# Row softmax on one core: tiles of 15, 7 and 3 rows per partition in place of 16, 8 and 4

## The chip, the core and the metric

The kernel runs on one NeuronCore of a Trainium2 chip. Its engines have instruction streams of their own and meet only at semaphores: VectorE (DVE in the profile) reduces and multiplies, ScalarE (ACT) computes exponentials, SyncE (SP) only issues transfers here. Sixteen DMA engines move data between HBM and the on-chip memory SBUF, which has 128 partitions. Transfers issued by ACT go through one queue (q10 in the profile), those issued by SP through another (q1); both run on the same sixteen engines. The metric is the device time of one execution in microseconds (us).

## The reference

A softmax over the last axis, at temperature 2, of 16 x 1024 rows of 512 float32 numbers:

```python
temp = 2.0
x_scaled = x / temp
x_max = np.max(x_scaled, axis=-1, keepdims=True)
exp_x = np.exp(x_scaled - x_max)
return exp_x / np.sum(exp_x, axis=-1, keepdims=True)
```

The input has 33.55 MB and so has the output; each is moved once. A row has 2 KB.

## The kernel before

There are 16,384 rows, 128 for each partition. A *tile* is a run of rows in HBM: tile t with r rows per partition takes 128 x r consecutive rows, and partition p gets the r consecutive ones from p x r on (`dram`, L54 to L56). A tile is therefore one contiguous stretch of HBM, cut into 128 pieces of r x 2 KB, and these pieces start r x 2 KB apart: with r = 16, the pitch from one partition to the next is 32 KB; with 8, 16 KB; with 4, 8 KB.

`PLAN` (L10) lists eleven tiles as (rows, place). The place is an offset in `arena`, an SBUF buffer of 100 rows per partition (L36), in which everything is computed in place. The first eight tiles (4, 8, five of 16, 8) fill the 100 rows exactly. The last three (16, 8, 4) reuse the places of tiles 2, 1 and 0; `behind` (L63 to L68) lists for each of them which earlier tile holds its place.

The work runs as follows.

- ACT issues the loads of the first eight tiles at the start (L81), one after another, and then computes.
- A *chunk* is 4 rows of a tile (`CHUNK`, L15), 32 in all. For chunk k, DVE takes the negated maximum of each row (L99, one instruction per chunk, `do_max`), ACT computes exp(0.5 x - max) row by row and accumulates the row's sum (L84, four instructions), and DVE takes the reciprocals (L108) and multiplies each row by its own (L112, `do_mul`).
- DVE's order is max(k), then mul(k - 2), since `LAG` is 2 (L121 to L125). The max of a tile's chunks waits for that tile's load.
- SP stores tile t when its last chunk is multiplied (L130, L131). After store t it issues the loads of late tiles whose place was held by tile t - 2 or an earlier one; each first waits for the store of that earlier tile (L132 to L136). In this plan all three late loads are issued after store 4. At the end SP waits for all stores (L137, L138).

SP's queue is first in, first out: a late load stands behind the stores issued before it.

Of the kernel before, what the change touches and what calls it, by code (L numbers as in the profile page):

```python
# [1 line left out]

# [4 lines left out]

PLAN = [  # L10
    (4, 0), (8, 4), (16, 12), (16, 28), (16, 44), (16, 60), (16, 76),
    (8, 92), (16, 12), (8, 4), (4, 0),
]
ARENA = 100
CHUNK = 4  # L15
LAG = 2


@with_exitstack
def kernel(  # L20
    ctx: ExitStack,
    tc: tile.TileContext,
    x: bass.AP,
    out: bass.AP,
):
    nc = tc.nc
    fp32 = mybir.dt.float32

    xf = x.flatten_outer_dims()
    of = out.flatten_outer_dims()  # L30
    N, D = xf.shape
    P = nc.NUM_PARTITIONS
    n_rows = N // P
    assert sum(r for r, _ in PLAN) == n_rows

    arena = nc.alloc_sbuf_tensor("arena", (P, ARENA, D), fp32)  # L36
    negmax = nc.alloc_sbuf_tensor("negmax", (P, n_rows), fp32)
    sums = nc.alloc_sbuf_tensor("sums", (P, n_rows), fp32)
    recip = nc.alloc_sbuf_tensor("recip", (P, n_rows), fp32)


    tiles, base = [], 0
    for r, at in PLAN:
        tiles.append((base, r, at))
        base += r

    chunks = [
        (t, b + c, at + c)
        for t, (b, r, at) in enumerate(tiles)
        for c in range(0, r, CHUNK)  # L50
    ]
    last_chunk = {t: k for k, (t, _, _) in enumerate(chunks)}

    def dram(ap, t):  # L54
        b, r, _ = tiles[t]
        return ap[b * P : (b + r) * P].rearrange("(p r) d -> p r d", r=r)  # L56

    def sb(t):
        _, r, at = tiles[t]
        return arena[:, at : at + r, :]  # L60


    behind = {}  # L63
    for t, (_, r, at) in enumerate(tiles):
        for u in range(t):
            _, ru, au = tiles[u]
            if at < au + ru and au < at + r:
                behind.setdefault(t, []).append(u)  # L68

    with tc.tile_critical():  # L70
        ld = [tc.alloc_semaphore(f"ld{t}") for t in range(len(tiles))]
        st = [tc.alloc_semaphore(f"st{t}") for t in range(len(tiles))]
        s_max = tc.alloc_semaphore("s_max")
        s_exp = tc.alloc_semaphore("s_exp")
        s_rec = tc.alloc_semaphore("s_rec")
        s_mul = tc.alloc_semaphore("s_mul")


        for t in range(len(tiles)):
            if t not in behind:  # L80
                nc.scalar.dma_start(out=sb(t), in_=dram(xf, t)).then_inc(ld[t], 16)  # L81
        for k, (t, b, a) in enumerate(chunks):
            for r in range(CHUNK):
                ins = nc.scalar.activation(  # L84
                    out=arena[:, a + r],
                    in_=arena[:, a + r],
                    func=mybir.ActivationFunctionType.Exp,
                    bias=negmax[:, b + r : b + r + 1],
                    scale=0.5,
                    accum_out=sums[:, b + r : b + r + 1],  # L90
                )
                if r == 0:
                    ins._wait_ge(s_max, k + 1)
            ins.then_inc(s_exp, 1)


        def do_max(k):
            t, b, a = chunks[k]
            nc.vector.reduce_max(  # L99
                out=negmax[:, b : b + CHUNK],  # L100
                in_=arena[:, a : a + CHUNK],
                axis=mybir.AxisListType.X,
                negate=True,
            )._wait_ge(ld[t], 16).then_inc(s_max, 1)

        def do_mul(k):
            t, b, a = chunks[k]
            nc.vector.reciprocal(  # L108
                out=recip[:, b : b + CHUNK], in_=sums[:, b : b + CHUNK]
            )._wait_ge(s_exp, k + 1).then_inc(s_rec, 1)  # L110
            for r in range(CHUNK):
                ins = nc.vector.tensor_scalar_mul(  # L112
                    out=arena[:, a + r],
                    in0=arena[:, a + r],
                    scalar1=recip[:, b + r : b + r + 1],
                )
                if r == 0:
                    ins._wait_ge(s_rec, k + 1)
            ins.then_inc(s_mul, 1)

        for k in range(len(chunks) + LAG):  # L121
            if k < len(chunks):
                do_max(k)
            if k >= LAG:
                do_mul(k - LAG)  # L125


        late = sorted(behind)
        for t in range(len(tiles)):
            nc.sync.wait_ge(s_mul, last_chunk[t] + 1)  # L130
            nc.sync.dma_start(out=dram(of, t), in_=sb(t)).then_inc(st[t], 16)  # L131
            while late and max(behind[late[0]]) <= t - 2:  # L132
                u = late.pop(0)
                for v in behind[u]:
                    nc.sync.wait_ge(st[v], 16)
                nc.sync.dma_start(out=sb(u), in_=dram(xf, u)).then_inc(ld[u], 16)  # L136
        for t in range(len(tiles)):  # L137
            nc.sync.wait_ge(st[t], 16)  # L138


# [1 line left out]
_INS = ['x']  # L142
_OUTS = [((16, 1024, 512), 'float32')]


# [23 lines left out]
```

The softmax here doesn't subtract the row's maximum and nothing guards it: scores larger than these inputs give would overflow.

## Time and profile before

| What | Value |
|---|---|
| device time, median of 4 runs | 164.23 us (163.81 to 165.01) |
| the profiled execution's own time | 163.81 us |
| its span | 162.0 us |
| moved by DMA | 67.14 MB, mean 414 GB/s over the span |
| DMA issues | 8 loads from ACT, 3 loads and 11 stores from SP |
| DVE max of a chunk (L99) | 32 x 2280 ns, 72.9 us |
| DVE multiply of a row (L112) | 128 x 482 ns, 53.6 us |
| ACT exponential of a row (L84) | 128 x 710 ns, 90.8 us |
| DVE waits for loads | 15.1 us in 5 waits, the first of them 5.64 us at the start |
| SP waits for DVE before stores | 133.2 us in 11 waits |

The durations come from one profiled execution, whose span runs from its first to its last recorded instruction; about 1.8 us of the device time lie around it. The page gives each engine's busy time, a row of forty slices in which a digit is the busy share in tenths, and for each DMA queue the number of packets, the megabytes and the time that its packets took, as a share of the span of sixteen engines. Busy times of neighbouring instructions on one engine can overlap by some tens of ns, so a sum over means can be a little above the time that passes. Idle time of an engine that does not set the end costs nothing.

### The profile page before, as it was taken

To read this page: it belongs to the slowest core of one execution; us is meant where nothing else is said; L and a number is where in the kernel's file an instruction comes from. 1 tells how busy PE (TensorE), PEld (TensorE's weight loads), DVE (VectorE), ACT (ScalarE), POOL (GpSimd) and SP (SyncE) were. 2 spreads that over 40 slices of the span, in tenths; PEclk is the share of its full clock that TensorE was granted. 3 is DMA by queue.
4 is the path that set the end of the run, shared out by engine and by line. 5 is a ranking of instruction groups with operands and counts; after the bars stand their busy time and mean duration, and the time that the engine had idled before them with its cause. 6 is when DMAs were issued, how large, how long until landed. Compare 5 with 4: busy or idle time off the path is not lost.

```text
span 162.0 us, 528 instructions
## 1 busy us (share of the span) xinstructions
DVE 127.0 (78%) x192; ACT 95.0 (59%) x257; POOL 0.2 (0%) x4
## 2 busy tenths in 40 slices
DVE  0539199999999999999985999998999999930000
ACT  0368537777777777777771777776777777700000
POOL 0000000000000000000000000000000000000000
DMA  5999989999999999999999999999999999999993
GB/s 166 433 437 502 404 344 459 453 417 396 421 483 396 445 445 404 437 421 437 413 453 409 441 425 443 421 429 400 417 429 445 445 413 407 429 461 429 400 423 148
DMA packets 3172, 67.14 MB, mean 414 GB/s; under 512 B 352, under 2 KB 352, under 8 KB 352
## 3 DMA queue, kind: packets, MB, share of 16 engines
q1 hardware_dynamic: 2016, 40.90, 59.1%
q10 hardware_dynamic: 1152, 26.21, 38.4%
q14 instruction: 4, 0.03, 0.0%
HBM read 33.55 MB, written 33.55 MB: 414 GB/s over the span
## 4 chain that ended last, share of the span: by engine, by line
DVE 54%; DMA 33%; issue 1%; ACTq 1%; SPq 0%
DMA arena<-in_x_dram 33%; DVE negmax L99 29%; DVE arena L112 24%; DVE recip L108 1%; ACTq L81 1%; SPq L131 0%; ACTq L164 0%; SPq L70 0%
## 5 line engine op out<-in xcount | busy, mean ns | idle before, releaser
L84 ACT ACTIVATE arena<-arena,negmax 128x512 f32<-128x512 f32 x128 | 90.8, 710 | 40.7 <-DVE negmax L99 40.7
L99 DVE TENSOR_REDUCE negmax<-arena 128x4 f32<-128x2048 f32 x32 | 72.9, 2280 | 15.1 <-DMA arena<-in_x_dram 15.1
L112 DVE TENSOR_SCALAR arena<-arena,recip 128x512 f32<-128x512 f32 x128 | 53.6, 482 | 1.1
L84 ACT ACTIVATION_READ_ACCUMULATOR arena<-arena,negmax 128x1 f32 x128 | 23.9, 187 | 0.0
L108 DVE RECIPROCAL recip<-sums 128x4 f32<-128x4 f32 x32 | 5.4, 168 | 0.0
L84 ACT ACT_TABLE_LOAD x1 | 1.3, 1283 | 5.1 <-issue 5.1
L153 POOL MEMSET const-bfloat16-1.0<- 128x1 bf16 x1 | 0.1, 101 | 0.0
L153 POOL MEMSET const-uint8-127<- 128x1 uint8 x1 | 0.1, 101 | 0.0
L153 POOL MEMSET const-float32-0.0<- 128x1 f32 x1 | 0.1, 98 | 0.2 <-issue 0.2
L153 POOL MEMSET const-float32-1.0<- 128x1 f32 x1 | 0.1, 98 | 0.0
## 6 DMA issues: line engine op xcount, KB each, us to landing
out_dram<-arena SPq DMA_DIRECT2D x6, 4096.0 KB, 26.2
arena<-in_x_dram ACTq DMA_DIRECT2D x5, 4096.0 KB, 44.7
out_dram<-arena SPq DMA_DIRECT2D x3, 2048.0 KB, 20.1
arena<-in_x_dram ACTq DMA_DIRECT2D x2, 2048.0 KB, 53.3
arena<-in_x_dram SPq DMA_DIRECT2D x1, 4096.0 KB, 34.7
out_dram<-arena SPq DMA_DIRECT2D x2, 1024.0 KB, 17.4
arena<-in_x_dram SPq DMA_DIRECT2D x1, 2048.0 KB, 38.3
arena<-in_x_dram ACTq DMA_DIRECT2D x1, 1024.0 KB, 4.7
```

The lines of the kernel that those rows point to most:

```text
L81: nc.scalar.dma_start(out=sb(t), in_=dram(xf, t)).then_inc(ld[t], 16)
L84: ins = nc.scalar.activation(out=arena[:, a + r], in_=arena[:, a + r], func=mybir.ActivationFunctionType.Exp, bias=negmax[:, b + r : b + r ...
L99: nc.vector.reduce_max(out=negmax[:, b : b + CHUNK], in_=arena[:, a : a + CHUNK], axis=mybir.AxisListType.X, negate=True,)._wait_ge(ld[t], ...
L108: nc.vector.reciprocal(out=recip[:, b : b + CHUNK], in_=sums[:, b : b + CHUNK])._wait_ge(s_exp, k + 1).then_inc(s_rec, 1)
L112: ins = nc.vector.tensor_scalar_mul(out=arena[:, a + r], in0=arena[:, a + r], scalar1=recip[:, b + r : b + r + 1],)
L153: nc = _bacc.Bacc("TRN2", target_bir_lowering=False, num_devices=1)
```

## The change

The plan now gives each tile as a list of chunk sizes: tiles of 3, 7, six of 15, and at the end 15, 7, 3 and 3 rows. A tile of 15 has three chunks of 5 rows, one of 7 a chunk of 4 and one of 3, and one of 3 a single chunk. There are twelve tiles instead of eleven and 28 chunks instead of 32. The pitch from one partition to the next in HBM becomes 30, 14 or 6 KB. The first eight tiles again fill the 100 rows of `arena`. The late tiles are now four: tile 8 in the place of tile 2, tile 9 in that of 1, tile 10 in that of 0, and tile 11 (3 rows) in part of that of tile 3, so its load is issued after store 5. A chunk carries its own size, and the loops run over it.

```diff
 PLAN = [
-    (4, 0), (8, 4), (16, 12), (16, 28), (16, 44), (16, 60), (16, 76),
-    (8, 92), (16, 12), (8, 4), (4, 0),
+    ([3], 0), ([4, 3], 3), ([5] * 3, 10), ([5] * 3, 25), ([5] * 3, 40), ([5] * 3, 55),
+    ([5] * 3, 70), ([5] * 3, 85), ([5] * 3, 10), ([4, 3], 3), ([3], 0), ([3], 25),
 ]
 ARENA = 100
-CHUNK = 4
 LAG = 2
...
-    tiles, base = [], 0
-    for r, at in PLAN:
+    tiles, chunks, base = [], [], 0
+    for t, (cs, at) in enumerate(PLAN):
+        r = sum(cs)
         tiles.append((base, r, at))
+        o = 0
+        for c in cs:
+            chunks.append((t, base + o, c, at + o))
+            o += c
         base += r
-
-    chunks = [
-        (t, b + c, at + c)
-        for t, (b, r, at) in enumerate(tiles)
-        for c in range(0, r, CHUNK)
-    ]
-    last_chunk = {t: k for k, (t, _, _) in enumerate(chunks)}
+    last_chunk = {c[0]: k for k, c in enumerate(chunks)}
...
+    def do_max(k):
+        t, b, c, a = chunks[k]
+        nc.vector.reduce_max(
+            out=negmax[:, b : b + c],
+            in_=arena[:, a : a + c],
+            axis=mybir.AxisListType.X,
+            negate=True,
+        )._wait_ge(ld[t], 16).then_inc(s_max, 1)
...
-        for k, (t, b, a) in enumerate(chunks):
-            for r in range(CHUNK):
+        for k, (t, b, c, a) in enumerate(chunks):
+            for r in range(c):
```

`do_mul` changes in the same way: its reciprocal takes c numbers and its loop runs over c rows. The rest of the diff puts the loads of ACT into a function `issue_loads` and the rest into `compute_and_store`, which are called one after the other; the order of issue on each engine follows the same rules as before.

More of the change, by code (lines that the diff above doesn't have):

```diff
@@ L33 @@
     n_rows = N // P
-    assert sum(r for r, _ in PLAN) == n_rows
+    assert sum(sum(c) for c, _ in PLAN) == n_rows
     arena = nc.alloc_sbuf_tensor("arena", (P, ARENA, D), fp32)
@@ L68, with issue_loads, do_mul, compute_and_store @@
                 behind.setdefault(t, []).append(u)
[L70 to L79, printed above, removed]
+    ld = [tc.alloc_semaphore(f"ld{t}") for t in range(len(tiles))]
+    st = [tc.alloc_semaphore(f"st{t}") for t in range(len(tiles))]
+    s_max = tc.alloc_semaphore("s_max")
+    s_exp = tc.alloc_semaphore("s_exp")
+    s_rec = tc.alloc_semaphore("s_rec")
+    s_mul = tc.alloc_semaphore("s_mul")
+    def issue_loads(begin, end):
+        for t in range(begin, end):
             if t not in behind:
                 nc.scalar.dma_start(out=sb(t), in_=dram(xf, t)).then_inc(ld[t], 16)
-        for k, (t, b, a) in enumerate(chunks):
-            for r in range(CHUNK):
+    def do_max(k):
[6 more added lines that the diff above has]
+        )._wait_ge(ld[t], 16).then_inc(s_max, 1)
+    def do_mul(k):
+        t, b, c, a = chunks[k]
+        nc.vector.reciprocal(
+            out=recip[:, b : b + c], in_=sums[:, b : b + c]
+        )._wait_ge(s_exp, k + 1).then_inc(s_rec, 1)
+        for r in range(c):
+            ins = nc.vector.tensor_scalar_mul(
+                out=arena[:, a + r],
+                in0=arena[:, a + r],
+                scalar1=recip[:, b + r : b + r + 1],
+            )
+            if r == 0:
+                ins._wait_ge(s_rec, k + 1)
+        ins.then_inc(s_mul, 1)
+    def compute_and_store():
+        for k, (t, b, c, a) in enumerate(chunks):
+            for r in range(c):
                 ins = nc.scalar.activation(
@@ L94 @@
             ins.then_inc(s_exp, 1)
[L97 to L119, printed above, removed]
         for k in range(len(chunks) + LAG):
@@ L138 @@
             nc.sync.wait_ge(st[t], 16)
+    with tc.tile_critical():
+        issue_loads(0, len(tiles))
+        compute_and_store()
 _INS = ['x']
```

## The prediction

> **What bounds the kernel now.** I read the page first: the engines' busy times, the forty slices and the DMA queues.
>
> ```profile
> span 162.0 us, 528 instructions
> DVE 127.0 (78%) x192; ACT 95.0 (59%) x257; POOL 0.2 (0%) x4
> ...
> DMA  5999989999999999999999999999999999999993
> ...
> q1 hardware_dynamic: 2016, 40.90, 59.1%
> q10 hardware_dynamic: 1152, 26.21, 38.4%
> ```
>
> VectorE (DVE) is busy 78% of the span. The DMA row is full from the second slice to the last but one, and the two queues' packets took 59.1 + 38.4 = 97.5% of sixteen engines' span: 158.0 of 162.0 us. The other 4 us are the head (the first packet starts at 1.8 us) and the tail (the last byte lands at about 160.2). So DMA sets the end, although the chain of waits names DVE for 54%: a chain runs through whatever happened to be waited for, and DVE ends at 143.2, with 17 us of stores still queued.
>
> Next, the stretches of the trace: us, length, busy DVE, ACT and POOL with instructions, clock, share of DMA engines busy, GB/s.
>
> ```profile
> 2.00:16.00 14.00, 7.69 (x7) 7.33 (x18) 0.00 (x0) 1.00 1.00 417
> 24.00:157.00 133.00, 114.96 (x180) 83.84 (x230) 0.00 (x0) 1.00 1.00 428
> 145.00:157.00 12.00, 0.00 (x0) 0.00 (x0) 0.00 (x0) 1.00 0.97 418
> ```
>
> Loads alone (first row), the mixture (second) and stores alone (third) all run with the engines full at 417 to 428 GB/s. One row per partition (128 x 2 KB) read or written therefore costs 262,144 B / 428 GB/s = 0.6125 us, and 256 such rows cost 156.8.
>
> Then the records of single packets in the trace. A packet is one partition's contiguous run, 8, 16 or 32 KB: 22 transfers x 128 = 2816 of them, plus 22 x 16 semaphore writes of 9 ns. The most frequent duration of each size is also its minimum: 309, 611 and 1213 ns, which 2500 of the 2816 take. Doubling a packet adds 302 or 602, so a packet costs some 7 ns besides its bytes. The time above these minima, summed and divided by 16 engines, is the whole **excess** any better address pattern could win: 2.09 us. It splits into the first 4-row load (before the engines have settled) 0.51, the last 4-row load (114.6 to 119 us; mean 364 instead of 309) 0.44, 32 KB loads 0.80 (20 ns each), 32 KB stores 0.32 (6 ns each), rest 0.02.
>
> **The change, part by part.** My sum stands against the profiled execution, 163.81 (span 162.0 and 1.8 around it); the median of the four runs is 164.23, and I add the same difference to that.
>
> *The pitch.* Tiles remain one contiguous run of HBM; only where each partition's piece starts in it changes, 30 KB apart instead of 32. The engines' least packet times do not depend on the pitch before: 8, 16 and 32 KB pieces all move at 27 GB/s per engine. Between 8.5 and 13.5 us, loads at 32 KB pitch with nothing beside them, no packet is above its minimum; at the end of the kernel the same holds for stores. Bounds: a gain of at most 2.09 - 0.51 = 1.58 (the start-up share is not a matter of pitch), a loss not bounded by a row. I take 0 for the big tiles, the value of the undisturbed stretches. A rule is worth weighing here. The Trainium skill ("DMA: Bandwidth & Descriptors", section "Latency and other measured facts") has copies losing rate at large power-of-two row pitches: 207 GB/s per direction at 512 KiB against 214 in full. Read as "any power of two costs this", it would promise 3.3% of 157, 5.2 us. But it starts at sixteen times our pitch, and names contiguous tiles as an alternative cure, which this kernel has already; and our steady 428 GB/s, half in each direction, is its full rate. The row decides: 1.58 at most, not 5.2.
>
> *More, smaller transfers.* 12 tiles instead of 11 make 24 transfers instead of 22: per engine 16 more packets at 7 ns and 2 semaphore writes at 9 ns, 0.13 us. Here a rule speaks against the change: the same page ("Anatomy of one DMA") charges some 2.0 us fixed per transfer, which would be 4 us for two. The trace has transfers queued behind one another: from 1.8 to 160.2 us, engines are idle 158.4 - 157.8 = 0.6 us on average over all 22. The fixed part lies beside other transfers' packets while a queue is never empty; so 0.13, not 4.
>
> *The small loads.* Before has one 4-row load late in a full queue, with 0.44 us of excess; after has two of 3 rows (tiles 10 and 11). Nearest row: another 0.44; if it was chance, 0. I take half, 0.22.
>
> *Compute.* 32 chunks become 28. Four rows take DVE 2.19 + 0.12 + 1.68 = 3.99 us (max; reciprocal and gaps; four multiplies, in the chain of waits), five at most 5/4 of max and multiply: 2.74 + 0.12 + 2.09 = 4.95, so 0.99 per row instead of 1.00. ACT needs about 0.71 x 5 = 3.5 of these. All of that lies beside DMA: worth 0, provided a queue always holds something. That needs checking, because loads and stores move.
>
> *The supply of the queues.* ACT's queue still gets 100 rows at the start (3 + 7 + 6 x 15), so its issue is the same eight instructions. SP's order becomes stores 0 to 4, loads 8, 9, 10, store 5, load 11, stores 6 to 11; load 11 (new) waits for store 3, which was issued about 30 us before. In the FIFO of rows, and 1.8 us for the start: tile 2 lands after 25 rows and 3 of store 0, at 19.0 us (before: 20.5). Store 2 then goes out 23.4 us of DVE later, at 42.4; by then 66 rows have moved, 10 of them stores. From there stores share evenly with loads (0.816 rows per us each), so 85 loaded rows stand at 78 and 100 at 96.3. The same sum for before gives 86.4 for its tile 6, measured:
>
> ```profile
> 86.95 2.29 DVE L99 TENSOR_REDUCE negmax<-arena 128x4 f32<-128x2048 f32 x1 [2.55 <-DMA arena<-in_x_dram]
> ```
>
> DVE wants tile 6 at 76.9 and tile 7 at 93.2 (three chunks of 4.95 after tile 6): it waits some 1.5 and 3.6 us, against 2.55 and 0.58 before, the second wait now at tile 7 because that tile has 15 rows, not 8. Tile 8 is wanted at 111.6 and lands at 106. DVE ends at about 144 (before 143.2). What matters is whether store 8 is issued before store 7 has drained. Before:
>
> ```profile
> 135.60 0.33 SPq L131 DMA_DIRECT2D out_dram<-arena  x1
> ```
>
> and stores to tile 7 drain at 1.8 + 228 x 0.6125 = 141.4: cover of 5.8 us. After: issued at 134.7, needed at 141.6, cover 6.9. Store 6: issued 106.7, needed 123. So no queue runs dry, DVE's new wait costs nothing, and a last store of 3 rows instead of 4 drains under the same tail.
>
> **Sum.** 0 (pitch) + 0.13 + 0.22 + 0 (compute) = +0.35: 163.81 becomes 164.16 in a profiled run, and 164.23 becomes 164.58. I forecast **164.5**, no change that can be told: about 0.5% (0.8 us) is what a measurement of this kernel can tell from none, with four runs 1.2 us apart. Its own range is 163.5 to 165.2.
>
> **Rivals.**
> *A, the pitch does cost.* The 32 KB loads' excess and the 4-row loads' late excess are collisions in HBM, and 30 and 6 KB pitches spread them: 164.23 - 1.58 + 0.13 = 162.8. For it: the excess sits in loads, at certain times, many packets at once. Against: long stretches at the same pitch have none, and 1.58 is the ceiling.
> *B, slower: the new pitch collides more.* Place: the 112 packets of 30 KB per engine (14 transfers x 8). Before, sixteen engines step through pieces a power of two apart; that may be the good pattern. If every 30 KB packet, stores too, gets the 20 ns of the 32 KB loads, excess of large tiles is 2.24 instead of 1.12; with 0.13 and 0.44 that is +1.7: 165.9. It decides from 6 ns more per packet (0.82 - 0.13 = 0.69 us over 112). For it: 8 KB loads in a full queue took 18% more at the one place where they occur. Against: stores at 8, 16 and 32 KB all sit on the minimum.
> *C, a queue runs dry.* If tile 7 comes 7 us later than I have it, store 8 is late and each further us is a us of the end: 10 us later, 167.6.
> *D, it does not do what it says.* If 30 KB does not go as one packet but in pieces of 16, 8, 4 and 2, three more per packet at 7 ns are 112 x 3 x 7 ns = 2.35 us: 166.9. Nothing in this trace shows a size that is not a power of two, so it cannot be excluded.
>
> **How the numbers follow.** Forecast 0.48 (0.45 of it within 0.5%, 0.03 slower), A 0.20, B 0.22, C 0.05, D 0.05. Faster 0.20, same 0.45, slower 0.35. The range 162.6 to 166.3 takes in A's 162.8 and B's 165.9 with some room and leaves out the far side of B, most of C and D.
>
> **What would show it.** In the changed profile: the DMA row full but for its ends, and 24 x 144 = 3456 packets in the two queues (D: more). Packets of 30 KB with a most frequent time of 7 + 30/32 x 1206 = 1138 ns, 6 KB near 234, 14 KB near 535, and an excess near 2.3 us (A: under 1; B: over 3). The steady rate 426 to 429 GB/s. DVE's waits for loads at tiles 6 and 7 near 1.5 and 3.6 us. Store 8 issued near 135 and no slice below 9 at 141 (C). The forecast is wrong if the packets' minima move, or if the shares fall below 9 tenths anywhere between the ends.

## The result, and the profile after

| | median | runs |
|---|---|---|
| before | 164.43 us (163.54 to 167.99) | 55 |
| changed | 163.61 us (163.0 to 164.32) | 36 |

The ratio is 0.9955, 95% interval [0.9943, 0.9967]: faster by 0.45%, some 0.74 us. A later run of the same pair (e11) gives 0.9959 [0.9939, 0.9978]. The ratios leave out slow executions such as the one of 167.99. The effect is small but clear of the noise, and the forecast of no change, at 164.5, missed its direction.

The two profiled executions do not show it: the one of before took 163.81, below its median, the one of after 163.95, above its own. A difference of 0.45% has to be read from several profiles and from the intervals.

Page of the changed kernel: busy times, the DMA row of the forty slices and the DMA queues.

```profile
span 162.2 us, 523 instructions
DVE 126.2 (78%) x184; ACT 94.5 (58%) x257; POOL 0.2 (0%) x4
...
DMA  5999999999999999999999999989999999999992
...
q1 hardware_dynamic: 2304, 40.90, 58.8%
q10 hardware_dynamic: 1152, 26.21, 38.4%
q14 instruction: 3, 0.02, 0.0%
```

DMA is as full as before. The packets are 3456, so 30 KB go as one packet; in the packet records the most frequent times are 1138 ns for 30 KB, 535 for 14 and 234 for 6. The excess that was forecast near 2.3 us is 1.53. One more row differs: q14, instruction, has 3 packets here and 4 before.

Of the compute side, two lines of the timeline of VectorE in the changed kernel (start, duration, what, idle time before it and its cause), and SyncE's issue of store 8:

```profile
78.59 2.82 DVE L85 TENSOR_REDUCE negmax<-arena 128x5 f32<-128x2560 f32 x1 [1.75 <-DMA arena<-in_x_dram]
96.88 2.82 DVE L85 TENSOR_REDUCE negmax<-arena 128x5 f32<-128x2560 f32 x1 [3.41 <-DMA arena<-in_x_dram]
```

```profile
134.82 0.33 SPq L134 DMA_DIRECT2D out_dram<-arena  x1
```

The waits forecast at tiles 6 and 7 are there (1.5 and 3.6 us were expected), and store 8 goes out at 134.8 (134.7 expected). Nothing on the compute side reaches the end.

**Where the end comes from.** Each transfer is cut over sixteen engines, and the last store counts as landed when the slowest engine has finished. The last stretches of the kernel before, and then of the changed one (the last two columns are the share of the sixteen engines busy and GB/s):

```profile
157.00:159.00 2.00, 0.00 (x0) 0.00 (x0) 0.00 (x0) 1.00 0.95 401
159.00:160.00 1.00, 0.00 (x0) 0.00 (x0) 0.00 (x0) 1.00 0.47 197
160.00:161.00 1.00, 0.00 (x0) 0.00 (x0) 0.00 (x0) 1.00 0.02 8
```

```profile
157.00:159.00 2.00, 0.00 (x0) 0.00 (x0) 0.00 (x0) 1.00 0.87 366
159.00:160.00 1.00, 0.00 (x0) 0.00 (x0) 0.00 (x0) 1.00 0.18 74
160.00:161.00 1.00, 0.00 (x0) 0.00 (x0) 0.00 (x0) 1.00 0.02 6
```

Between 159 and 160 us, 0.47 x 16 = 7.5 engines are busy on average before (first fence), 0.18 x 16 = 3 after (second): most engines finish earlier, and a straggler or two keep the end where it was in this execution. The sixteen landings of the last store say the same: after, fourteen come by 159.70 and the last two at 160.37 and 160.66; before, seven come later than 159.90, the last at 160.52. The two stragglers of the changed kernel are there from the start: at the first load its last two landings trail the median landing by 0.7 us (0.6 in e11), where before none trails by more than 0.11 (0.12 in e12). Two landings trail in the same way at most transfers from there to the end. On one engine each packet starts where the one before ended; followed in this way, they are the same two engines, and no instruction fetch falls on either.

### The profile page after: what moved, and what is told of

Its sections match the earlier page's. It is cut to its first block, busy times and chain, and to the rows that moved or that the text cites. A ratio compares the mean times of both kernels' runs of the same rounds, so it can differ in the third digit from the quotient of the medians.

```text
span 162.2 us, 523 instructions
## 1 busy us (share of the span) xinstructions
DVE 126.2 (78%) x184; ACT 94.5 (58%) x257; POOL 0.2 (0%) x4
## 4 chain that ended last, share of the span: by engine, by line
DVE 74%; DMA 10%; another core or an unknown queue 3%; issue 1%; ACTq 1%; SPq 0%
DVE negmax L85 40%; DVE arena L98 32%; DMA arena<-in_x_dram 10%; DVE recip L94 2%; ACTq L81 1%; ACTq L171 0%; SPq L143 0%
## 5 line engine op out<-in xcount | busy, mean ns | idle before, releaser
L85 DVE TENSOR_REDUCE negmax<-arena 128x5 f32<-128x2560 f32 (+2 forms) x28 | 72.3, 2585 | 16.9 <-DMA arena<-in_x_dram 16.9
L94 DVE RECIPROCAL recip<-sums 128x5 f32<-128x5 f32 (+2 forms) x28 | 4.9, 175 | 0.0
```

Source lines behind the costliest of these rows:

```text
L85: nc.vector.reduce_max(out=negmax[:, b : b + c], in_=arena[:, a : a + c], axis=mybir.AxisListType.X, negate=True,)._wait_ge(ld[t], 16).the ...
L94: nc.vector.reciprocal(out=recip[:, b : b + c], in_=sums[:, b : b + c])._wait_ge(s_exp, k + 1).then_inc(s_rec, 1)
```

## The experiments

Excess is, as in the prediction, the time of the packets above the most frequent time of their size, per engine. It is taken from one profile for each kernel. The packets are given to transfers by their order in the queue and their size. Ratios are against the kernel before, run beside them on the same chip.

### Pitch or plan

e1 keeps the old tiles and takes their rows from larger groups, so that the pitch is 24 to 96 KB and no power of two (all of these are multiples of 8 KB, which the 30, 14 and 6 KB of the change are not); e2 does the opposite to the changed kernel (`GROUPS = [128]`, pitch 256 KB).

```diff
+GROUPS = [12, 48, 40, 28]
...
-        return ap[b * P : (b + r) * P].rearrange("(p r) d -> p r d", r=r)
+        g = max(x for x in range(len(GROUPS)) if sum(GROUPS[:x]) <= b)
+        g0, R = sum(GROUPS[:g]), GROUPS[g]
+        rows = ap[g0 * P : (g0 + R) * P].rearrange("(p r) d -> p r d", r=R)
+        return rows[:, b - g0 : b - g0 + r, :]
```

> The kernel before with its tiles of 16, 8 and 4 rows, chunks, order and packets of 32, 16 and 8 KB as they were; only the HBM rows that a tile covers are chosen so that the pitch from partition to partition is 24, 96, 80 or 56 KB (no power of two), and a tile is no longer one contiguous run. Theory P (a pitch that is no power of two spreads the loads over HBM and shortens the stretched packets): the gain of the change appears, ratio 0.994 to 0.997 against before, excess of the packets over their most frequent time at 1.6 us per engine or less. Theory E (the small tiles at the two ends did it): 0.999 to 1.001. Theory Z (the size of the large pieces, 30 instead of 32 KB, did it): 0.999 to 1.001.

> The changed kernel with its tiles of 15, 7 and 3 rows and its order, but the HBM rows of a tile chosen so that the pitch is 256 KB everywhere, a power of two; tiles are not contiguous. Theory P: the gain is gone or turned round, ratio 0.999 or more, excess 2.1 us per engine or more. E and Z: the gain stays, ratio 0.994 to 0.997.

e3 and e4 split the plan: small end tiles of the change with large tiles of 16 rows, and the reverse.

```diff
-    ([3], 0), ([4, 3], 3), ([5] * 3, 10), ...
+    ([3], 0), ([4, 3], 3), ([4] * 4, 10), ([4] * 4, 26), ([4] * 4, 42), ([4] * 4, 58),
+    ([4] * 4, 74), ([5, 5], 90), ([4] * 4, 10), ([4, 3], 3), ([3], 0), ([2], 26),
```

```diff
-    ([3], 0), ([4, 3], 3), ([5] * 3, 10), ...
+    ([4], 0), ([4, 4], 4), ([5] * 3, 12), ([5] * 3, 27), ([5] * 3, 42), ([5] * 3, 57),
+    ([5] * 3, 72), ([5, 4, 4], 87), ([5] * 3, 12), ([4, 4], 4), ([4], 0), ([1], 27),
```

> The changed kernel's small tiles (3, 7, and at the end 7, 3 and a last one of 2 rows) with large tiles of 16 rows as before (32 KB pitch and pieces), one of 10 to fill the buffer; everything contiguous. P and Z: nearly nothing is won, 0.998 to 1.001. E: the gain of the change is here, 0.994 to 0.997.

> Large tiles of 15 rows as in the changed kernel (30 KB pitch and pieces), small tiles of 4 and 8 rows as before, one of 13 to fill the buffer and a last one of 1 row; everything contiguous. P and Z: the gain of the change is here, 0.994 to 0.997. E: 0.999 to 1.001.

| kernel | ratio | excess | instruction fetches before the last packet |
|---|---|---|---|
| e1, old tiles, odd pitch | 0.9994 [0.9978, 1.0009] | 1.89 | 4 |
| e2, new tiles, 256 KB | 0.9995 [0.9971, 1.0019] | 1.64 | 3 |
| e3, 16 rows, small ends new | 1.0024 [1.0008, 1.0041] | 1.68 | 4 |
| e4, 15 rows, small ends old | 0.9987 [0.9971, 1.0004] | 1.80 | 3 |

e1 speaks against the pitch: without its powers of two the old kernel wins nothing. e2 speaks for it in time, since the gain is gone and nothing but the pitch was changed. Its profile says where: 0.85 of its 1.64 us sit in the first load (0.31 in the changed kernel), and the rest, 0.79, is less than the 1.22 of the changed kernel. So the packets of the large tiles are not stretched more at a pitch of 256 KB. The stretch with the first load, of e2 and then of the changed kernel:

```profile
2.00:6.00 4.00, 0.65 (x1) 0.80 (x1) 0.00 (x0) 1.00 0.97 346
```

```profile
2.00:6.00 4.00, 0.67 (x1) 0.76 (x1) 0.00 (x0) 1.00 1.00 391
```

Neither half of the plan shows the gain alone: e4's interval reaches from 1.0004 down to 0.9971, and e3 is even slower, outside all that was expected. The excess does not order these times either: e3 has 1.68, hardly more than the changed kernel. The kernel before has 192 VectorE instructions, the changed one 184. The column at the right shows that kernels with 192 or more VectorE instructions fetch instructions once more before the end.

### The instruction fetch

The packets of q14 have 8 KB and run on the same sixteen engines. The packet records show what one does: in the kernel before, the fetch at 135.0 us takes 0.309, in place of the engine's next data packet, and that packet then takes 0.351 longer than its kind. e1 and e3 have the same there (0.374 and 0.358).

e5 has the transfers of before with fewer VectorE instructions; e6 gives VectorE of the changed kernel some more, behind its last multiply, whose results nobody reads.

```diff
+    ([4], 0), ([4, 4], 4), ([6, 5, 5], 12), ([6, 5, 5], 28), ([6, 5, 5], 44), ([6, 5, 5], 60),
+    ([6, 5, 5], 76), ([4, 4], 92), ([6, 5, 5], 12), ([4, 4], 4), ([4], 0),
```

```diff
+        pad = nc.alloc_sbuf_tensor("pad", (P, 16), fp32)
+        for i in range(16):
+            nc.vector.memset(pad[:, i : i + 1], 0.0)
```

> All transfers of the kernel before (tiles of 16, 8 and 4, pitch, packets, order), but a tile of 16 rows is computed in chunks of 6, 5 and 5 instead of four of 4, so VectorE has 180 instructions instead of 192. In the profiles so far every kernel with 192 or more has a fourth 8 KB instruction fetch at about 135 us between the data packets of one DMA engine (0.31 us, and the packet after it 0.35 us longer); those with 184 have only three in that stretch. Theory F (the fourth fetch holds up the engine that ends last): fetch gone, ratio 0.995 to 0.998. Theories P and E (pitch; small tiles at the ends): fetch may go, 0.999 to 1.001.

> The changed kernel with 16 one-column memsets on VectorE behind its last multiply, which nothing waits for: 200 instructions. F: the fourth fetch comes back before the last packet and with it the time, 0.998 to 1.001 against before. P and E: the gain stays, 0.994 to 0.997.

e6: 0.9978 [0.9962, 0.9994], between the two forecasts. By the ratios half of the gain is gone, but the interval just overlaps that of the changed kernel (to 0.9967). The DMA queues between 130 and 145 us (packets, MB, share of sixteen engines) of the changed kernel and then of e6:

```profile
q1 hardware_dynamic: 244, 6.51, 100.7%
```

```profile
q1 hardware_dynamic: 243, 6.48, 100.4%
q14 instruction: 1, 0.01, 0.1%
```

The fetch is back, at 139.7 us. In this profile one engine lands at 161.16, the next at 160.28. The landings of the stores show that the fetch did it: at store 6, just before it, the last landing trails the median by 1.30 us, at store 7 and to the end by 2.0 to 2.1.

e5: 1.0012 [0.9985, 1.0038]. Its fetch is gone from the stretch (the fourth comes at 163.8), and there is no gain. This is a miss for the theory as I had put it: a fetch less helps only if the engine that carries it would be last. In e5's profile all sixteen landings lie within 159.61 to 160.33; there the time is set by what delays all of them.

The landings say the same of the kernel before. Its fetch falls between the landings of stores 5 and 6, and the lag of the last landing behind the median goes from 0.78 to 0.70 us there; in e12 from 1.42 to 1.31, in e1 from 1.68 to 1.69. The fetch delays an engine that is not the last, so in these profiles the kernel before would not have ended earlier without it. In e3 it hits one of four engines that already trail by 2.3 us: 2.45 becomes 3.26, and that engine ends the kernel.

To see fetches at work on a larger scale I added about four, early, in the changed kernel:

```diff
+        pad = nc.alloc_sbuf_tensor("pad", (P, 512), fp32)
+        for i in range(512):
+            nc.gpsimd.memset(pad[:, i : i + 1], 0.0)
```

> The changed kernel with 512 one-column memsets on GpSimd at the start, which nothing waits for: about four more 8 KB instruction fetches through the DMA engines. Theory F (a fetch holds its engine up by 0.31 us and stretches the packet behind it by some 0.35, and the end waits for the last engine): if they go to one engine, its landings trail the others by 1.5 to 3 us from then on and the ratio is 1.003 to 1.012; if spread over engines, 0.997 to 1.002. If fetches do not count at all: 0.994 to 0.997 as before the memsets.

> The changed kernel once more, for a second profile and as the control of the others of this call: 0.994 to 0.997; three fetches before the last packet, excess 1.5 to 1.6, first load 0.3, stores of tiles 3 and 4 together under 0.1.

1.0042 [1.0021, 1.0064], where the changed kernel beside it (e11) has 0.9959: 0.83% or 1.4 us for four fetches by the ratios, 1.1 us by the two medians (164.93 and 163.82). The page of e9 and its tail:

```profile
POOL 8795730000000000000000000000000000000000
...
q14 instruction: 7, 0.06, 0.1%
```

```profile
159.00:160.00 1.00, 0.00 (x0) 0.00 (x0) 0.00 (x0) 1.00 0.19 80
160.00:162.00 2.00, 0.00 (x0) 0.00 (x0) 0.00 (x0) 1.00 0.07 28
```

GpSimd is busy in the first six slices only (first line), and nothing waits for it. (VectorE's busy time is 130.4 us here against 126.2, but that holds no transfer up: fifteen engines land by 160.18, in the changed kernel by 160.37.) Yet at the other end of the kernel, for two microseconds, 0.07 x 16 = 1.1, so one engine works nearly alone. Its last landing is at 162.36, that of the next at 160.18. Already at tile 2, landing at 18 to 20 us, one engine trails the median by 1.85 us. What this engine loses early it does not make up: its lag is still there at every later load and at the end.

### The first load

> The changed kernel with its first tile contiguous (6 KB pitch), all others in one group with a pitch of 250 KB. Theory L (the packets of the first load are stretched: 0.85 us of excess per engine at 256 KB pitch, 0.5 with 4 contiguous rows, 0.3 with 3, and this start delays all engines alike; the pitch of the others is without effect): the gain is back, 0.992 to 0.997, first load at 0.3. If non-contiguous large tiles cost the gain: 0.998 to 1.001.

The edit is the one of e2 with `GROUPS = [3, 125]`. 0.997 [0.9949, 0.9992], first load 0.15, total 1.32, the lowest of all profiles. The direction is the forecast one, so the first load can account for e2; the intervals of e2 and e10 overlap, so this is indicated and not shown. It tells little of the change itself: the changed kernel's first load has 0.31 and 0.43 in two profiles, that of before 0.51 and 0.57.

### The late small load

In the kernel before the load of tile 10, 4 rows, was stretched most (0.44). e7 puts three such loads in a row, e8 four of 3 rows.

The cuts of e7, e8 and e13 to e15 are set against the plan of before, written in the notation of the changed kernel; that of e16 against the changed plan.

```diff
-    ... ([4] * 4, 12), ([4, 4], 4), ([4], 0),
+    ... ([4] * 4, 12), ([4], 4), ([4], 8), ([4], 0),
```

```diff
-    ... ([4] * 4, 12), ([4, 4], 4), ([4], 0),
+    ... ([4] * 4, 12), ([3], 4), ([3], 7), ([3], 0), ([3], 28),
```

> The kernel before with its last 28 rows as 16, 4, 4, 4 instead of 16, 8, 4: three late loads of 4 rows (1 MB, 8 KB pitch) instead of one; 32 chunks, 192 VectorE instructions. Theory E (late 4-row loads are stretched, some 0.3 to 0.4 us of mean excess each): slower, 1.003 to 1.010, excess in 110 to 125 us of about 1 us per engine. F and P: 0.999 to 1.002.

> As the kernel with three late 4-row loads, but with four of 3 rows (0.75 MB, 6 KB pitch) in their place. E: no stretch there (under 0.2 us of excess in all four), 0.996 to 1.000. F and P: 0.999 to 1.002, the same as with the 4-row loads.

Both theories of size fall: in e7 the three loads have 0.00, 0.01 and 0.36, in e8 those of 3 rows 0.00, 0.04 and 0.64, and the fourth, behind store 5, 0.00. It is always the one in front of store 5. Times 1.0007 [0.9984, 1.0029] and 1.0008 [0.999, 1.0026]. Four more kernels take that apart: the last two tiles exchanged (e13), 3 rows and 1 in place of 4 (e14), tile 5 of 15 rows in the old plan (e15) and of 16 in the new one (e16).

```diff
-    ... ([4, 4], 4), ([4], 0),
+    ... ([4], 0), ([4, 4], 4),
```

```diff
-    ... ([4, 4], 4), ([4], 0),
+    ... ([4, 4], 4), ([3], 0), ([1], 28),
```

```diff
-    ... ([4] * 4, 60), ([4] * 4, 76), ([4, 4], 92), ...
+    ... ([4, 4, 4, 3], 60), ([4] * 4, 75), ([5, 4], 91), ...
```

```diff
-    ... ([5] * 3, 55), ([5] * 3, 70), ([5] * 3, 85), ...
+    ... ([6, 5, 5], 55), ([5] * 3, 71), ([5, 5, 4], 86), ...
```

> The kernel before with its last two tiles exchanged: late loads of 16, 4, 8 rows instead of 16, 8, 4. If the last late load, the one in front of store 5 in the queue, is stretched whatever its size: load of tile 10 (8 rows) 0.2 us or more of excess per engine, load of tile 9 (4 rows) under 0.05. If it is a matter of the 4-row size: tile 9's 0.2 or more, tile 10's under 0.05. Time 0.998 to 1.003.

> The kernel before with the last tile of 4 rows split into 3 and 1, the 1-row load behind store 5: the load in front of store 5 now has 3 rows, all else as before. If 3 rows instead of 4 are the cure: excess of tile 10's load under 0.15 and 0.998 to 1.000; if not, 0.3 to 0.7 and 1.000 to 1.003.

> The kernel before with tile 5 of 15 rows and tile 7 of 9: the store behind the last late load has pieces of 30 KB instead of 32. If the piece of the store behind matters: excess of tile 10's load (4 rows) under 0.15; if not, 0.26 to 0.70 as in the kernels so far. Time 0.997 to 1.002.

> The changed kernel with tile 5 of 16 rows and tile 7 of 14: the store behind the late 3-row load has pieces of 32 KB. If the piece of the store behind matters: excess of tile 10's load 0.2 or more, ratio 0.996 to 0.999; if not, under 0.15 and 0.994 to 0.997.

| kernel | ratio | load in front of store 5 | its excess |
|---|---|---|---|
| e13 | 0.9997 [0.9964, 1.003] | 8 rows, store of 16 behind | 0.77 (the 4-row load before it 0.00) |
| e14 | 1.0007 [0.9976, 1.0038] | 3 rows, 16 | 0.65 |
| e15 | 0.9997 [0.9968, 1.0026] | 4 rows, 15 | 0.39 |
| e16 | 0.998 [0.9959, 1.0001] | 3 rows, 16 | 0.08 |

Stretches of e13 around that load:

```profile
113.00:115.00 2.00, 1.97 (x4) 0.87 (x3) 0.00 (x0) 1.00 1.04 446
115.00:117.00 2.00, 2.00 (x4) 2.00 (x6) 0.00 (x0) 1.00 1.08 393
117.00:119.00 2.00, 1.97 (x4) 0.94 (x4) 0.00 (x0) 1.00 1.04 352
119.00:121.00 2.00, 2.00 (x4) 2.00 (x6) 0.00 (x0) 1.00 1.06 459
```

These are the same columns as in the tails above. The engines count as fully busy throughout (1.04 to 1.08) while the rate falls from 446 to 352 GB/s and comes back: longer packets, no empty queue. A busy share alone would hide that. The same stretch in the changed kernel:

```profile
111.00:113.00 2.00, 2.00 (x3) 2.00 (x7) 0.00 (x0) 1.00 1.20 498
113.00:115.00 2.00, 1.96 (x3) 0.70 (x3) 0.00 (x0) 1.00 1.06 458
115.00:117.00 2.00, 2.00 (x6) 2.00 (x7) 0.00 (x0) 1.00 0.96 415
```

e16's interval covers both 1 and the changed kernel's ratio, so its time tells nothing; its packets do. Neither the load's size nor the pieces of the store behind it decide. Over all profiles, each kernel that begins with tiles of 4 and 8 has 0.26 to 0.77 in the load in front of store 5, e4 with its 15-row tiles included (0.32), and each that begins with 3 and 7 has 0.01 to 0.15, e3 with its 16-row tiles included (0.13). The two groups differ as well in where all later tiles lie in the buffer and in HBM (from row 12 on in the one, from row 10 on in the other), and no run separates that from the first two tiles. What does this 110 us later was not tried and stays open.

Last, before once more:

> The kernel before once more, for a second profile: 0.999 to 1.001; four fetches, excess 1.8 to 2.9, first load 0.5, stores of tiles 3 and 4 together 0.1 to 0.7.

1.0001 [0.9978, 1.0023], 4 fetches, excess 2.33, load in front of store 5 0.70, stores 3 and 4 together 0.28, first load 0.57: as expected.

## Why the prediction was wrong

**What held.** DMA sets the end and nothing of compute reaches it; the packets' counts and least times, the two new waits, store 8's time and the cover of the queues came as worked out. The 0.13 us for more packets are in the minima: 155.81 us per engine after, 155.66 before. For the large tiles no run shows a price of the pitch in their packets, and a pitch that is no power of two (e1) or 30 KB for the large tiles alone (e4) brings no gain that can be told. The Trainium skill's rule on large power-of-two pitches ("DMA: Bandwidth & Descriptors", section "Latency and other measured facts") begins at 512 KiB with a loss of 7 in 214 GB/s; e2, at half of that, shows no longer packets in its large tiles. That the start-up share "is not a matter of pitch" did not hold in e2, whose first load has 0.85 us.

**What failed.** The sum had +0.35 us, measured is -0.74. There are three profiles with the transfers of before (before, e12, e5) and four with those of after (after, e11, e6, e9). Mean excess per engine, us:

| | before | after | difference | my term |
|---|---|---|---|---|
| load in front of store 5, and the 3-row load behind it | 0.50 | 0.10 | -0.40 | +0.22 |
| stores 3 and 4 | 0.21 | 0.01 | -0.20 | 0 |
| first two loads | 0.54 | 0.49 | -0.05 | 0 |
| loads 2 to 7 | 0.84 | 0.93 | +0.09 | 0 |
| all | 2.16 | 1.60 | -0.56 | +0.22 |

1. *The small loads: the step that failed.* "Nearest row: another 0.44; if it was chance, 0. I take half, 0.22" priced one stretched load as a cost per small load. e7 and e13 show that it belongs to the place in front of store 5, once per kernel, and in the new plan it nearly vanishes. The term is -0.40 and has the wrong sign: my bounds went from none to another 0.44, and not below none.
2. *The large tiles at zero.* "I take 0 for the big tiles" used stretches that were undisturbed, although the prediction's own list has 0.80 us of excess in 32 KB loads and 0.32 in 32 KB stores (so those stores do not "all sit on the minimum", as is said against rival B). Stores 3 and 4, written while loads run, cost 0.20 less in the new plan, and loads 2 to 7 cost 0.09 more.
3. *The measure itself.* I divided the excess by 16 and treated the result as time. That holds for what delays all engines. A delay of one engine counts in full if that engine is last, and not at all if it is not. e3 shows it best: its median landing of the last store, 158.79, is earlier than in the changed kernel (159.15 and 159.04 in two profiles), but four engines come 2.3 us or more later, and it is slower than before. In the changed kernel two engines that are late from the first load on set the end; the third last lands at 159.70, 0.96 us before the last.

Together the packets give -0.56 + 0.16 (more packets, semaphore writes) = -0.40 of the measured -0.74. These are means over engines and few profiles, so even that part is no exact account of the end, and the other 0.34 is not accounted for.

4. *A term that I gave no thought.* The fourth instruction fetch. Its row (q14) was on the page, and I did not ask what 192 against 184 VectorE instructions would fetch. It looks like the missing part: e6 puts it at 0.9978 - 0.9955 = 0.23%, some 0.38 us. But that size is rough, and two things speak against counting it for the kernel before. e5 takes the fetch out and its interval leaves at most 0.15% of gain; and in both profiles of before the engine that is last is not the one that the fetch delays. What is shown is that a fetch can cost time where it falls on the last engine (e6, e3, e9).

Two readings of the prediction were off without moving the sum. The section "Anatomy of one DMA" of the Trainium skill's page "DMA: Bandwidth & Descriptors" states its 2.0 us for transfers that GpSimd issues, and those here are issued by ACT and SP, so only the row of the trace (0.6 us idle over 22 transfers) bore on that step. And the 0.80 us of the 32 KB loads, spread over all six of them, are 17 ns for each packet, not 20.

Rival A had the direction, but for a reason that e1 and e4 do not bear out, and its 162.8 was too low; B, C and D did not happen.

**Open.** The 0.34 us that the packets leave. Why plans that begin with tiles of 3 and 7 spare a load 110 us later; why stores 3 and 4 are cleaner with the new plan; why two engines are late at a first load of 3 rows, and why four trail at the end of e3. Whether the pitch of 256 KB costs e2 its gain through the first load alone.

## What to carry to other kernels

Where every transfer is cut over sixteen engines and none makes up what it lost, the end is the slowest engine's: look at the spread of the last landings and not only at the mean busy share. Count the small things that ride on the same engines, instruction fetches among them: a few instructions more on an engine that sets nothing can put one into the stream, and it costs time if it falls on the engine that is last. And before believing that a layout constant did it, give that constant alone to the old kernel.

## What the runs showed of the hardware

- An instruction fetch is an 8 KB packet of 0.309 us in the data stream of one DMA engine, and the packet after it took 0.35 to 0.37 us longer in three kernels with a fetch near 135 us (before, e1, e3). Four fetches from GpSimd made one engine end 2.2 us behind the next in e9.
- A GpSimd program that nothing waits for, done within 25 us, lengthened a kernel of 164 us by 1.1 to 1.4 (e9 against e11).
- A packet's least time is some 7 ns and 27 GB/s per engine for pieces of 2 to 32 KB alike: 84 ns for 2 KB (e14), 159 for 4 and 761 for 20 (e3), 234 for 6, 535 for 14 and 1138 for 30 (after).
